# Ten steps later: when an expert stage makes its copies of x and gathers the next group

## The chip, the cores and the metric

One core of a Trainium2 chip runs the whole program. The metric is the device time of one execution in microseconds (us); where several runs were made, their median.

## The reference, cut to what matters

Two blocks follow each other on one sequence of 256 tokens with 1024 features, all in float32. The first block (two layers of neighbourhood and differential attention) is not touched. The second block has two layers:

```
for i in range(2):                       # layer 0: sparse attention, layer 1: latent attention
    proj = x @ w_in
    mix  = nsa_mixer(...) or mla_mixer(...)             # 12 heads
    xa   = memory_cross_attention(xq, mk, mv)           # 4 heads, 256 columns
    x    = layer_norm(ALPHA * x + concat(mix, xa) @ w_out[i])
    # 16 experts in 4 groups; each token goes to 2 of them
    f    = sum over experts e of gate_e * (silu(x @ w_gate[e]) * (x @ w_up[e])) @ w_down[e]
    x    = layer_norm(ALPHA * x + f)
```

One expert has w_gate and w_up (1024 x 512 each) and w_down (512 x 1024): 6 MiB of weights. Sixteen experts in two layers make 192 MiB, each byte read once.

## The kernel before, in words

**Order.** The order on TensorE (PE), VectorE (DVE) and ScalarE (ACT) is written out by hand. In the expert stage (`moe`) it goes by numbered steps: expert e has the sixteen steps from 16e, and at every odd step 16e + 2k + 1 the matmuls of feature block k (`Expert.mm(k)`, gate and up) are issued. `at(pre, s, fn)` puts other work ahead of step s, `at(post, s, fn)` behind it. Nothing waits for a step as such: each engine works through its own list and waits only for data and for free buffers.

**What stands around the experts.** Expert e's `gate1` to `hidden2` (ACT and DVE) run at 16e + 16 to 16e + 20, its two halves of `down` (PE) at 16e + 27 and 16e + 35, `result1` and `result2` at 16e + 37 and 16e + 38. Four experts share one group. For every group after the first, the tokens are gathered by matmul (`gather`, from `xs`, the two float32r parts of x, and from the one-hot matrices `Dg`, with four matmuls per feature block) into `xg`, and `back` makes `dT` and the gates. `hots` fills Dg in two calls. `x_parts` makes `xs` (one ACT copy and one DVE subtraction for each of four pieces of 128 x 512), from `xn`. `open_expert` puts the next group's pieces at steps counted from s = 16e of experts 2, 6 and 10.

**Buffers for weights.** The weights come in pieces of 512 KB, issued on the queue of SyncE (SP) into three kinds of buffers: `ring` (12 of one piece), `b8` (8 slots of two pieces) and `b4` (19 slots of one piece). b8 and b4 also hold the activations: xn, xg, xs, f are b8; Dg, dT, the experts' results ys are b4. When the last reader of a weight buffer has been issued, `Weights.read` frees it and, if `Weights.may` agrees, loads the next pieces of a fixed order into free slots at once. `may` looks ahead: `others` lists the steps at which the stage will take (+) or give back (-) slots for activations, and a free slot is refilled only if, at each of those steps, enough slots are free or come free (`last`, the step of a buffer's last reader) before it:

```
for s, n in self.others[kind]:
    if s >= self.step:
        free -= n
        if free + sum(e < s for e in ends) < 0:
            return False
```

In layer 0 the SP queue's order is the written one; in layer 1 SP is not in the hand-written schedule, and its loads are ordered by the framework's scheduler.

**The layer before the second expert stage** (`mla_layer`) goes by steps of another counter (`Flow`). The cross attention's result `xo` (128 x 2 x 256) is split into two float32r parts by `split_to` (one ACT copy, one DVE subtraction for each half) as feature blocks 6 and 7 of `yT`, which feeds the output projection.

Of the kernel before, what the change touches and what calls it, by code (L numbers as in the profile page):

```python
# [32 lines left out]
class Emit:  # L33


    def __init__(self, ctx, tc, aps, manual=False, nring=12, n8=8, n4=19, nw=3):
        self.tc, self.nc, self.a = tc, tc.nc, aps
        pool = lambda name, bufs, **kw: ctx.enter_context(tc.tile_pool(name=name, bufs=bufs, **kw))
        self.const = pool("const", 1)
        self.ring = pool("ring", nring)  # L40
        self.p8 = pool("p8", 1)
        self.p4 = pool("p4", 1)
        self.work = pool("work", 2)
        self.small = pool("small", 2)
        self.psum = pool("psum", 1, space=PSUM)
        self.slots = {"b8": list(range(n8)), "b4": list(range(n4)), "bank": list(range(8))}
        self.taken = {}
        self.lead = nw
        if manual:
            ctx.enter_context(tc.manual_schedule())  # L50
        nc = self.nc
        self.ident = self.const.tile([P, P], F32, name="ident")
        make_identity(nc, self.ident)
        self.sel = self.const.tile([P, 20], F32, name="sel")
        nc.vector.tensor_reduce(self.sel, self.ident.rearrange("p (j c) -> p c j", j=4)[:, :20], axis=AX.X, op=OP.add)
        self.mhalf = self.const.tile([P, 16], F32, name="mhalf")
        nc.vector.memset(self.mhalf, -0.5)
        self.one = self.const.tile([P, 1], F32, name="one")
        nc.vector.memset(self.one, 1.0)
# [1529 lines left out]
def mla_layer(E, x, f, st, flow, mkv, first, fill, W):  # L1589
# [3 lines left out]
    t = {}  # L1593
# [259 lines left out]
    for half in range(2):  # L1853
        s = 29 + 7 * half
# [9 lines left out]
    h0 = 34  # L1864
    yT = []
# [30 lines left out]
                                 m.pT[:, S * i:S + P * i], start=i == 0, stop=i == 1, skip_group_check=True)  # L1896
        E.free(*(m.pT for m in ms))

    def new_yT():
        yT.append(E.new_T("yT"))  # L1900
        for i in range(2):
            E.split_to(yT[0], 6 + i, t["xo"][:, i])
        E.free(t["xo"])

    flow.before(h0 + 8, new_yT)
    for j in range(6):
        ms = [Head(E, None, None, 2 * j + b, b, None) for b in range(2)]
        for m in ms:
            s = h0 + m.i
# [217 lines left out]
class Weights:  # L2127
# [3 lines left out]
    def __init__(self, E, i):  # L2131
        self.E, self.i, self.m = E, i, [E.a[n][i] for n in ("moe_w_gate", "moe_w_up", "moe_w_down")]
        self.pieces = {(e, w): [] for e in range(NE) for w in range(3)}
        self.order = []
        for e in range(NE):
            at = ((e, 0), (e, 1), *[(e - 2, 2)] * 2, *[(e, 0), (e, 1)] * 2, *[(e - 1, 2)] * 2, (e, 0), (e, 1))
            self.order += [p for p in at if p[0] >= 0 and p != (NE - 2, 2)]
        self.order += [(NE - 2, 2)] * 4 + [(NE - 1, 2)] * 4
        self.unread, self.ring = {}, []


        self.early = [(1, 0), (1, 0)]
        self.step, self.last = 0, {"b8": {}, "b4": {}}
        self.others = {"b8": [(28, 2), (64, -1), (88, 1)], "b4": [(11, 1), (13, -1)]}
        for s in (30, 94, 158):
            self.others["b4"] += [(s, 1), (s + 7, 1), (s + 19, 1), (s + 23, 1), (s + 30, -1), (s + 39, 1), (s + 55, 1)]
            self.others["b4"] += [(s + 62, -5)]
            self.others["b8"] += [(s + 69, 1), (s + 98, -1)]
        self.others["b4"] += [(226, 1), (229, 2), (232, 1), (235, 1), (238, -4), (245, 1), (257, 2)]
        if i == 0:  # L2150
            self.others["b8"].append((16 * NE - 19, 1))
            self.others["b4"].append((16 * NE - 19, 9))
        for v in self.others.values():
            v.sort(key=lambda e: (e[0], -e[1]))
# [207 lines left out]
def moe(E, x, i, W, st, columns, sums, tail=None, overflow=True):  # L2362
# [17 lines left out]
    def new_hots(m):  # L2380

        return E.b4((2, m, 2 * CAP), "Dg", F32R)

    def hots(Dg, slots, h, j=0, ts=range(2)):
        m = slots.shape[2]
        for t in ts:
            nc.vector.tensor_tensor(Dg[:, t, j:j + m, h * CAP:h * CAP + CAP],
                                    E.iota[:, None, :].to_broadcast([P, m, CAP]),
                                    slots[:, t, :, None].to_broadcast([P, m, CAP]), op=OP.is_equal)

    def new_group(m=n):

        return E.b8((KD, m, CAP), "xg"), []

    def new_back(g, m=n):
        ga = small.tile([P, n], F32, name="gall", tag="gall")
        g[1][:] = None, ga

        def new_dT():
            g[1][0] = E.b4((m, S), "dT", F32R)  # L2400
            return g[1][0]

        return new_dT, ga
# [6 lines left out]
    pre, post = {}, {}  # L2410

    def at(when, s, fn):
        when.setdefault(s, []).append(fn)

    def piece(s, gen, delay=2, m=1):

        def run():
            for k in range(m):
                out = next(gen)
                if delay:  # L2420
                    at(pre, s + delay + k, out)
                else:
                    out()
        at(post, s, run)

    groups, experts, ys = {}, {}, {}
    made = {}

    def open_expert(e):
        s, j, g = 16 * e, e % n, e // n  # L2430
        xg, matrices = groups[g]
        X = experts[e] = (Expert if e < NE - 1 else LastExpert)(E, [W.pieces[e, w] for w in range(3)], W.read, xg, j,
                                lambda: matrices[1][:, j:j + 1])
        if j == 2 and e + 2 < NE:
            slots = slot[:, :, e + 2:e + 2 + n]

            def start():
                made["Dg"] = new_hots(n)
                hots(made["Dg"], slots, 0)

            def gen():
                yield from gather(E, made["xs"], made["Dg"], groups[g + 1][0])
                yield from back(E, made["Dg"], E.gates, n * (g + 1), *new_back(groups[g + 1]))

            it = gen()
            at(pre, s - 2, start)
            at(pre, s + 3, lambda: groups.__setitem__(g + 1, new_group()))

            for d, m in ((3, 4), (17, 2)):
                piece(s + d, it, m=m)  # L2450
            at(pre, s + 14, lambda: hots(made["Dg"], slots, 1))
            at(post, s + 28, lambda: E.free(made["Dg"]))
        if j == n - 1:
            at(pre, s + 16, lambda: E.free(xg))
        if e == NE - 1:
            return
        for d, fn in ((16, X.gate1), (17, X.gate2), (18, lambda: X.hidden1(0)), (19, lambda: X.hidden1(1)),
                      (20, X.hidden2)):
            at(pre, s + d, fn)
        if e == NE - 2:  # L2460
            return
        for d in range(2):
            at(post, s + 27 + 8 * d, lambda d=d: X.down(d))
        at(pre, s + 37, X.result1)
        at(pre, s + 38, X.result2)
        at(pre, s + 39, lambda: ys.setdefault(g, []).append(X.y))
        if j == n - 1:
            def gen(f):
                yield from combine(E, f, ys.pop(g), matrices[0], range(n), None if g else made["xs"])

            def start():
                if g == 0:
                    made["f"] = E.b8((2, D), "f")
                it = gen(made["f"])
                piece(s + 44, it, m=4)
                at(post, s + 44, lambda: E.free(matrices[0]))

            at(pre, s + 40, start)

    with tc.manual_schedule(engines=ENGINES if i else ENGINES | {mybir.EngineType.SP}):  # L2480
# [3 lines left out]
        xn = E.b8((2, D), "xn")  # L2484
        negate, shift, choose, slots, gates1, gates2 = router(E, lg, mv, r, *sums)
# [6 lines left out]
        Dg = new_hots(n)  # L2492
# [32 lines left out]
        def x_parts(t, c):  # L2525
            if "xs" not in made:
                made["xs"] = E.b8((2, D), "xsh", F32R), E.b8((2, D), "xsl", F32R)
            hi, lo, src = (v[:, t, c] for v in (*made["xs"], xn))
            nc.scalar.copy(hi, src)
            nc.vector.tensor_sub(lo, src, hi)  # L2530
# [9 lines left out]
                at(pre, 9 + 2 * m + t, lambda t=t, c=c, j=j: gain(t, c, j))  # L2540
        for k in range(4):
            t, c = k % 2, slice(512 * (k // 2), 512 * (k // 2) + 512)
            at(pre, 28 + 0 * k, lambda t=t, c=c: x_parts(t, c))
        at(pre, 35, lambda: E.free(xn))

        ps, work = {}, ()

# [22 lines left out]
        for s in range(16 * NE + 2):  # L2570
            W.step = s
            e, k = divmod(s, 16)
# [57 lines left out]
    if overflow:  # L2630
        with tc.If(most > CAP, label=f"overflow{i}"):
            with tc.For_i(0, NE, 1) as e:
# [12 lines left out]
                for b in range(1, S // CAP):  # L2645
                    nc.vector.tensor_scalar(sl, sl, -float(CAP), None, op0=OP.add)
                    Dg = new_hots(1)
                    hots(Dg, sl, 0)
                    hots(Dg, sl, 1)
                    g = new_group(1)  # L2650
# [4 lines left out]
                    for w, k, c in ((wg, D, FF), (wu, D, FF), (wd, FF, D)):  # L2655
                        p = E.wload(rows(w, k) if c == D else rows8(w), k, c)
                        m = 1024 // c
# [101 lines left out]
def body(tc, aps, out):  # L2759
    nc = tc.nc  # L2760
    with ExitStack() as ctx:
# [17 lines left out]
        with tc.manual_schedule(engines=ENGINES):  # L2779
            x = E.b8((2, D), "x")  # L2780
            end = mla_layer(E, x, f, st, Flow(E, E.lead - 1), mkv, first, fill, W)
# [33 lines left out]
```

## Time and profile before

| what | us |
|---|---|
| median of 3 runs | 1001.55 |
| lowest, highest run | 998.66, 1002.4 |
| the profiled execution's own time | 998.92 |
| its span, first to last instruction | 997.2 |

The profiled execution lies 2.63 us below the median of the runs, and 1.72 us of its time lie outside the span. Times in the trace are counted from the span's start. Layer 0's expert stage runs from about 440 to 657 us, layer 1's from about 766 to 984. A busy share of PE in the profile is modelled: a matmul that stands waiting for its weights can count as busy, so the number of matmuls in a window tells more than its busy time.

### The profile page before, as it was taken

What the parts mean: (1) busy time and instruction counts of PE and PEld (TensorE: products, weight loads), DVE (VectorE), ACT (ScalarE), POOL (GpSimd) and SP (SyncE); (2) the same over time, 40 slices, a digit from 0 to 9 for tenths busy, and PEclk for the clock granted to TensorE, in tenths of its full rate; (3) what the DMA queues carried; (4) which work ended last, traced back from release to release, by engine and by line L of the source; (5) the groups of instructions that cost most, each with busy time, mean ns of one, the idle gap of its engine ahead of it and who ended that gap; (6) DMA issues with size and microseconds to landing.
All of it is one profiled execution on the core that took longest, in us unless ns stands there. A gap on an engine that the chain in (4) does not pass through costs nothing. (4 is left out here: it accounts for less than half of the span.)

```text
span 997.2 us, 16112 instructions
## 1 busy us (share of the span) xinstructions
PE 971.9 (97%) x5627; PEld 640.3 (64%) x5627; DVE 641.6 (64%) x1826; ACT 435.7 (44%) x1088; POOL 19.4 (2%) x40
## 2 busy tenths in 40 slices
PE   8999999999999989999999999999999999999995
PEld 8897889888897866775343443378867443434332
DVE  5857886557967788767456544467875645654455
ACT  6556664566664467653212121143875321212111
POOL 0000000000100000000000000000000000000000
PEclk9999999999999999999999999999999999999998
DMA  8963575443576584698999999977698899999995
GB/s 286 366 242 127 176 233 175 149 138 116 160 227 210 150 216 127 223 379 291 379 409 409 409 409 408 404 279 264 215 345 304 285 347 406 409 409 409 409 408 191
DMA packets 110889, 286.66 MB, mean 287 GB/s; under 512 B 14224, under 2 KB 30928, under 8 KB 110288
## 3 DMA queue, kind: packets, MB, share of 16 engines
q1 hardware_dynamic: 110800, 285.55, 79.8%
q8 instruction: 47, 0.77, 0.3%
q14 instruction: 42, 0.34, 0.1%
HBM read 284.46 MB, written 1.05 MB: 286 GB/s over the span
## 5 line engine op out<-in xcount | busy, mean ns | idle before, releaser
L2234 PE MATMUL eg<-wa,xg 128*64 128x512 f32 x792 | 204.9, 597 | 1.1 <-DMA wa<-moe_w_up_dram 0.8
L135 DVE TENSOR_TENSOR wsp<-w,wsp 128x512 fp32r<-128x512 f32 (+4 forms) x256 | 164.6, 656 | 64.0 <-ACT wsp L134 61.7
L253 PE MATMUL pj<-xTh,wsp 128*128 128x256 f32 x768 | 154.1, 291 | 1.7 <-ACT xTh L350 0.7
L134 ACT CAST wsp<-w 128x512 fp32r<-128x512 f32 (+4 forms) x256 | 142.3, 593 | 12.9 <-PE pj L253 5.7
L253 PEld LDWEIGHTS pj<-xTh,wsp 128*128 128x128 f32 x768 | 123.6, 191 | 9.0 <-issue 4.4
L2234 PEld LDWEIGHTS eg<-wa,xg 128*64 128x64 f32 x792 | 60.2, 137 | 107.1 <-issue 91.2
L2241 ACT ACTIVATE z<-eg 64x512 f32<-64x512 f32 x32 | 18.9, 592 | 210.2 <-PE eg L2234 210.2
L253 PE MATMUL pj<-xTl,wsp 128*128 128x256 f32 x384 | 108.6, 283 | 0.1
L253 PE MATMUL pj<-wsp,xTh 128*128 128x512 f32 (+3 forms) x352 | 108.5, 389 | 0.0
L2244 DVE SCALAR_TENSOR_TENSOR z<-z,eg 64x512 f32<-64x512 f32 x32 | 21.7, 679 | 127.6 <-ACT z L2241 127.6
L2254 DVE SCALAR_TENSOR_TENSOR hq<-z,gall,eg 32x128 f32<-32x128 f32 x240 | 83.4, 348 | 4.0
L2274 PE MATMUL dn<-wa,hT 128*64 128x512 f32 x348 | 83.8, 593 | 0.0
L253 PE MATMUL pj<-wsp,yTh 128*128 128x512 f32 x240 | 77.7, 405 | 0.0
L253 PEld LDWEIGHTS pj<-xTl,wsp 128*128 128x128 f32 x384 | 73.4, 191 | 0.7 <-DVE xTl L352 0.3
L2234 PE MATMUL eg<-w,xg 128*64 128x512 f32 x232 | 71.4, 595 | 0.2 <-DMA w<-moe_w_gate_dram 0.2
L253 PEld LDWEIGHTS pj<-wsp,xTh 128*128 128x128 f32 x352 | 62.8, 188 | 11.7 <-issue 2.5
L2285 ACT CAST ys<-dn 64x512 fp32r<-64x512 f32 x60 | 34.8, 580 | 75.5 <-PE dn L2274 65.5
L253 PE MATMUL pj<-wsp,xTl 128*128 128x512 f32 (+3 forms) x176 | 66.7, 379 | 0.0
L2274 PEld LDWEIGHTS dn<-wa,hT 128*64 128x64 f32 x348 | 24.7, 137 | 50.0 <-issue 42.7
L405 ACT ACTIVATE z<-z,mx 128x256 f32<-128x256 f32 (+1 forms) x104 | 48.1, 467 | 15.9 <-DVE mx L396 15.8
L2290 DVE TENSOR_TENSOR ys<-dn,ys 64x512 fp32r<-64x512 f32 x60 | 41.3, 689 | 12.3 <-ACT ys L2285 11.1
L253 PEld LDWEIGHTS pj<-wsp,yTh 128*128 128x128 f32 x240 | 43.1, 188 | 9.1 <-issue 1.6
(423 smaller groups left out, 1428.9 us busy)
## 6 DMA issues: line engine op xcount, KB each, us to landing
wa<-moe_w_up_dram SPq DMA_DIRECT2D x101, 512.0 KB, 10.2
wa<-moe_w_gate_dram SPq DMA_DIRECT2D x97, 512.0 KB, 10.2
wa<-moe_w_down_dram SPq DMA_DIRECT2D x93, 512.0 KB, 10.2
w<-w_in_dram SPq DMA_DIRECT2D x63, 512.0 KB, 5.0
w<-moe_w_down_dram SPq DMA_DIRECT2D x35, 512.0 KB, 10.2
w<-moe_w_gate_dram SPq DMA_DIRECT2D x31, 512.0 KB, 10.2
w<-moe_w_up_dram SPq DMA_DIRECT2D x27, 512.0 KB, 10.2
w<-w_out_dram SPq DMA_DIRECT2D x24, 512.0 KB, 3.6
```

Of the source, the lines that this page charges most:

```text
L134: self.nc.scalar.copy(hi, src)
L135: self.nc.vector.tensor_sub(lo, src, hi)
L253: nc.tensor.matmul(o, a, b, start=begin and i == 0, stop=last and i == 2, skip_group_check=True)
L405: E.nc.scalar.activation(z[i], (src or z)[i], AF.Exp, bias=mx[:, i:i + 1], scale=1.0 if src else -1.0, accum_out=sm[:, i:i + 1])
L2234: self.E.nc.tensor.matmul(self.ps[b * CAP:b * CAP + CAP], self.xg[:, k, self.j], w, start=k == 0, stop=k == KD - 1, skip_group_check=True)
L2241: self.E.nc.scalar.activation(self.th, self.ps[:CAP], AF.Tanh, scale=0.5)
L2244: self.E.nc.vector.scalar_tensor_tensor(self.th, self.th, 1.0, self.ps[:CAP], op0=OP.add, op1=OP.mult)
L2254: self.E.nc.vector.scalar_tensor_tensor(self.hq[32 * q:32 * q + 32, :, h], th[:, q], self.gate()[r], u[:, q], op0=OP.mult, op1=OP.mult)
L2274: self.E.nc.tensor.matmul(self.pd[n * CAP:n * CAP + CAP], self.hT[:, k], self.w[2][k](0)[:, 512 * n:512 * n + 512], start=k == 0, stop=k == 3,
L2285: self.E.nc.scalar.copy(self.y[r, n], self.pd[r])
L2290: self.E.nc.vector.tensor_sub(self.y[o, n], self.pd[r], self.y[r, n])
```

## The change

Three things move; no arithmetic changes, and the same instructions are issued.

- `x_parts`: the four pieces at step 28 go to steps 39, 40, 41 and 42, and xn is given back at 44, not 35.
- The next group's pieces (experts 2, 6, 10, steps from s = 16e): Dg taken and half filled at s + 10, not s - 2; xg taken at s + 13, not s + 3; the four gather pieces at s + 13, not s + 3; Dg's other half at s + 18, not s + 14; the two `back` pieces at s + 21, not s + 17; Dg given back at s + 22, not s + 28. The lists `others` follow.
- `mla_layer`: the two halves of xo are split at steps h0 + 7 and h0 + 9, not both at h0 + 8; yT's two b8 slots are taken one step earlier and xo's b4 slot is freed one step later.

```
-    def new_yT():
-        yT.append(E.new_T("yT"))
-        for i in range(2):
-            E.split_to(yT[0], 6 + i, t["xo"][:, i])
-        E.free(t["xo"])
-    flow.before(h0 + 8, new_yT)
+    def new_yT(i):
+        if i == 0:
+            yT.append(E.new_T("yT"))
+        E.split_to(yT[0], 6 + i, t["xo"][:, i])
+        if i == 1:
+            E.free(t["xo"])
+    for i in range(2):
+        flow.before(h0 + 7 + 2 * i, new_yT, i)
...
-        self.others = {"b8": [(28, 2), (64, -1), (88, 1)], "b4": [(11, 1), (13, -1)]}
+        self.others = {"b8": [(39, 2), (64, -1), (88, 1)], "b4": [(11, 1), (13, -1)]}
         for s in (30, 94, 158):
-            self.others["b4"] += [(s, 1), (s + 7, 1), (s + 19, 1), (s + 23, 1), (s + 30, -1), (s + 39, 1), (s + 55, 1)]
+            self.others["b4"] += [(s + 7, 1), (s + 12, 1), (s + 23, 2), (s + 24, -1), (s + 39, 1), (s + 55, 1)]
             self.others["b4"] += [(s + 62, -5)]
-            self.others["b8"] += [(s + 69, 1), (s + 98, -1)]
+            self.others["b8"] += [(s + 79, 1), (s + 98, -1)]
...
-            at(pre, s - 2, start)
-            at(pre, s + 3, lambda: groups.__setitem__(g + 1, new_group()))
-            for d, m in ((3, 4), (17, 2)):
+            at(pre, s + 10, start)
+            at(pre, s + 13, lambda: groups.__setitem__(g + 1, new_group()))
+            for d, m in ((13, 4), (21, 2)):
                 piece(s + d, it, m=m)
-            at(pre, s + 14, lambda: hots(made["Dg"], slots, 1))
-            at(post, s + 28, lambda: E.free(made["Dg"]))
+            at(pre, s + 18, lambda: hots(made["Dg"], slots, 1))
+            at(post, s + 22, lambda: E.free(made["Dg"]))
...
-            at(pre, 28 + 0 * k, lambda t=t, c=c: x_parts(t, c))
-        at(pre, 35, lambda: E.free(xn))
+            at(pre, 39 + k, lambda t=t, c=c: x_parts(t, c))
+        at(pre, 44, lambda: E.free(xn))
```

## Rows read from the trace of the kernel before

**Rows 1.** Windows of 25 us: stretch, PE, PEld, DVE, ACT, POOL busy, clock, DMA, GB/s.
```profile
575.00:600.00 25.00, 25.00 (x121) 8.95 (x121) 11.28 (x30) 5.29 (x11) 0.00 (x0) 1.00 1.03 409
600.00:625.00 25.00, 24.68 (x106) 9.81 (x104) 11.12 (x25) 4.42 (x8) 0.00 (x0) 1.00 1.03 409
625.00:650.00 25.00, 24.60 (x99) 8.74 (x96) 11.30 (x23) 3.59 (x7) 0.00 (x0) 1.00 1.03 397
...
950.00:975.00 25.00, 24.61 (x98) 9.05 (x98) 11.79 (x26) 4.64 (x8) 0.00 (x0) 1.00 1.03 405
```

**Rows 2.** PE's timeline late in layer 0's stage: start, length, what, idle before.
```profile
631.55 1.07 PE L2234 MATMUL eg<-wa,xg 128*64 128x512 f32 x2 [0.20 <-DMA wa<-moe_w_up_dram]
```

**Rows 3.** DMA issues from 495 to 640: count, KB, median us to landing.
```profile
DMA packets 16254, 59.27 MB, mean 409 GB/s; under 512 B 1804, under 2 KB 1804, under 8 KB 16245
...
wa<-moe_w_up_dram SPq DMA_DIRECT2D x24, 512.0 KB, 10.2
```

**Rows 4.** The SP queue's waits from 455 to 492: total us, times, longest.
```profile
SPq L2194 <- PE eg L2234: 18.2, 9, 5.7
```

**Rows 5.** Windows of 5 us, layer 0, columns as in Rows 1.
```profile
465.00:470.00 5.00, 5.00 (x24) 1.44 (x20) 3.41 (x10) 0.59 (x1) 0.00 (x0) 1.00 0.95 348
470.00:475.00 5.00, 5.00 (x40) 4.28 (x40) 3.50 (x8) 3.51 (x6) 0.00 (x0) 1.00 1.02 360
475.00:480.00 5.00, 5.00 (x26) 1.68 (x24) 0.00 (x0) 0.00 (x0) 0.00 (x0) 1.00 0.99 361
480.00:485.00 5.00, 5.00 (x28) 2.17 (x26) 3.05 (x8) 1.79 (x5) 0.00 (x0) 1.00 0.98 337
485.00:490.00 5.00, 5.00 (x26) 1.69 (x24) 2.58 (x9) 1.16 (x2) 0.00 (x0) 1.00 1.03 411
```

**Rows 6.** Windows of 5 us, layer 1, columns as in Rows 1.
```profile
790.00:795.00 5.00, 5.00 (x26) 1.64 (x24) 3.10 (x6) 2.77 (x5) 0.00 (x0) 1.00 0.94 316
795.00:800.00 5.00, 5.00 (x36) 3.56 (x33) 4.75 (x13) 2.34 (x4) 0.00 (x0) 1.00 0.79 270
800.00:805.00 5.00, 5.00 (x29) 2.26 (x29) 1.37 (x3) 1.17 (x2) 0.00 (x0) 1.00 0.90 267
805.00:810.00 5.00, 5.00 (x28) 2.14 (x26) 1.26 (x3) 1.32 (x4) 0.00 (x0) 1.00 1.02 379
810.00:815.00 5.00, 5.00 (x24) 1.61 (x24) 4.08 (x14) 1.63 (x4) 0.00 (x0) 1.00 0.96 302
```

**Rows 7.** DMA issues from 788 to 815, columns as in Rows 3.
```profile
wa<-moe_w_up_dram SPq DMA_DIRECT2D x5, 512.0 KB, 7.0
```

**Rows 8.** SP's timeline, layer 1: loads issued.
```profile
796.63 0.38 SPq L2194 DMA_DIRECT2D wa<-moe_w_gate_dram  x1
802.87 0.33 SPq L119 DMA_DIRECT2D w<-moe_w_down_dram  x1
...
814.37 0.33 SPq L2194 DMA_DIRECT2D wa<-moe_w_up_dram  x1
```

**Rows 9.** PE's timeline around layer 0's first gather (steps 35 to 43).
```profile
470.02 0.51 PE L2086 MATMUL xg<-Dg,xsh 128*128 128x256 f32 x2
...
474.05 3.65 PE L2234 MATMUL eg<-wa,xg 128*64 128x512 f32 x16
477.53 1.89 PE L2274 MATMUL dn<-wa,hT 128*64 128x512 f32 x8
```

**Rows 10.** DVE's timeline in the same stretch.
```profile
462.74 2.46 DVE L2530 TENSOR_TENSOR xsl<-xn,xsh 128x512 fp32r<-128x512 f32 x4
465.12 0.75 DVE L2387 TENSOR_TENSOR Dg<-iota,slot 128x256 fp32r<-128x256 f32 x2
...
471.46 1.39 DVE L2290 TENSOR_TENSOR ys<-dn,ys 64x512 fp32r<-64x512 f32 x2
```

**Rows 11.** Timeline at step h0 + 8 of layer 1's attention.
```profile
724.41 0.75 DVE L141 TENSOR_TENSOR yTl<-xo,yTh 128x256 fp32r<-128x256 f32 x2
...
725.71 0.61 PE L1883 MATMUL tp<-ident,z 128*128 128x128 f32 x3 [0.98 <-DVE z L164]
```

## The prediction

> **What bounds the kernel now.** I read the windows over the two expert stages first. In 575 to 600 PE issues 121 matmuls; after 600 it issues 106 and 99, and 98 late in layer 1, while memory stands at 409 GB/s [rows 1]. PE still looks 98% busy there, but its timeline shows matmuls that start behind a landing [rows 2]. So each stage ends on the weight stream: 512 KB at 409 GB/s are 1.28 us, and a landing 10.2 us after its issue is eight pieces in flight [rows 3]. In the second half of a stage nothing on PE, DVE or ACT moves the end; only an earlier stream does.
>
> Then I asked where the stream was late. Early in the stage the SP queue waits for PE to read a buffer before it may refill it: 18.2 us in nine waits from 455 to 492 [rows 4]. In that stretch memory is below its rate: 348, 360, 361, 337 GB/s in layer 0 until 485 [rows 5], and 316, 270, 267, 379, 302 in layer 1 until 815 [rows 6]. Afterwards it is full [rows 1, 5]. Against 409 the loss is (61 + 49 + 48 + 72) x 5 / 409 = 2.8 us in layer 0 and (93 + 139 + 142 + 30 + 107) x 5 / 409 = 6.2 us in layer 1. Whatever of this is recovered brings the end of the stage forward, as long as PE still waits at the end. How long it waits I estimate from the counts: (121 - 106 + 121 - 99) / 121 x 25 = 7.6 us in layer 0, an upper bound, since late work has other shapes; I take 5 us per layer as the cap.
>
> **The change, part by part.** *x's parts at 39, b8 slots.* The step promises two b8 slots for eleven steps more, but only if `may` can use them. I followed the fixed order of pieces by hand. In layer 0 the b8 weight tiles are read last at steps 11, 15, 19, 23, 59 and 63. The tiles of 19 and 23 were kept empty for xs at 28. Under the new list they stay empty until 39, since no other tile ends before 39. So in layer 0 this part frees nothing: 0. In layer 1 they end at 19, 27, 27, 35, 43 and 51. Before, both tiles of 27 stay empty and the tile of 35 is refilled; now one tile of 27 is refilled at once and the tile of 35 stays empty. Two pieces are issued eight steps earlier, and at 35 the count is the same again.
>
> *The later Dg, b4 slots.* In layer 0 one piece moves from step 39 to 31 (and one from 67 to 59, when the queue is full anyway). In layer 1 one moves from 35 to 23, one from 51 to 47, one from 63 to 55. Every one of these is a loan paid back within twelve steps.
>
> *The gather ten steps later.* It reads no weights and takes PE 474.05 - 470.02 = 4.0 us [rows 9]. Before, this pause lies ahead of step 37: in layer 1 the queue issues nothing from 796.63 to 802.87 [rows 8]. Now the reads of steps 37 to 45 come 4.0 us earlier and the pause lies ahead of 47. From 47 on PE is where it was (`back`, four steps later, gives step 51 some 2 us more), and the number of loads released is what it was.
>
> So the stream gains between the steps and is caught again by the same releases later. Ends of the estimate: nothing (caught wholly) and the whole loss (2.8 and 6.2 us). In layer 0 the reads after 485 already run at 411 GB/s [rows 5], so a piece gained there is kept: half of the bound, 1.4 us. In layer 1 releases still bind at 814.37 [rows 8], and a landing takes 7.0 us [rows 7], some five pieces; being ahead means fewer of them, and with a thin queue the rate was 267 to 302 [rows 6]. I take a quarter, 1.5 us. The later groups (steps 106 and 170) lie in the full stretch: 0; that cover is gone only if a stall there is longer than the eight pieces in flight, 10.2 us.
>
> *ACT and DVE at the new steps.* The x parts take DVE 2.46 us and half of Dg 0.75 [rows 10]. After the 1.39 us for ys, which ends at 472.85, they end at 472.85 + 2.46 + 0.75 = 476.06. PE reaches the moved gather after five blocks of mm (3.65 / 4 = 0.9 at most, 0.86 from start to start: (477.53 - 474.05) / 4 = 0.87) and one half down (1.7): 470.02 + 4.35 + 1.7 = 476.1 [rows 9, 10]. That is a tie. Bounds: 0, and 1 us a layer if ACT, which makes the high parts first, is late. I take 0.15 a layer, 0.3 in all. What queues behind x's parts on DVE is expert 2's hidden chain, which has until step 59.
>
> *xo in two steps.* DVE's two subtractions (0.75 us) at 724.41 stand before the scaling that PE waits 0.98 us for [rows 11]. Half of them goes a step earlier, where DVE is as full, and half a step later. Bounds: 0.75 saved, 0.4 lost; I take 0.4 saved. ACT's two copies move likewise and there the copy behind them waits for PE: 0.
>
> Sum: -1.4 - 1.5 + 0.3 - 0.4 = -3.0 us. Against the profiled execution's 998.92 that is 995.9; against the median of 1001.55, the number I forecast, 998.5.
>
> One rule speaks against any gain from the stream. The low windows stand at 337 to 361 GB/s in layer 0, the later ones at 409 [rows 5]. The Trainium skill's page "SBUF — State Buffer", section "Summary: rules for kernel authors", says to reckon with about 358 GB/s for transfers from HBM. By that the low windows of layer 0 would already be at memory's limit and its 1.4 us would be 0. This trace has 409 over 145 us [rows 3], so the rule doesn't hold here.
>
> **The rivals.**
> (1) *Caught wholly.* The loans are paid back and the same releases bind at steps 47 to 55; only xo and the tie are left: 0.1 us, 1001.4. For it: every moved load is repaid before the queue fills. Against it: rates in layer 0 are full directly afterwards.
> (2) *The stream keeps nearly all.* Layer 0 gives 2.8, layer 1 its cap of 5, xo 0.4: 8.2 us less, 993.3. For it: the queue's gap of 6.24 us [rows 8] goes just where memory is lowest. Against it: the pause is moved, not removed.
> (3) *Slower: the queue's head in layer 1.* SP's order there is the scheduler's. If it puts a piece whose slot is read after the moved gather ahead of pieces whose slots are free, all behind it wait. The longest wait for a read is 5.7 us [rows 4]; one such wait with no gain elsewhere costs 5.7 us, 1007.3. It decides from 3 us on, where it eats the forecast gain. Nothing in the trace shows that the order is disturbed by such shifts.
>
> **How the numbers follow.** Forecast 0.46, rival (1) 0.21, rival (2) 0.21, rival (3) 0.12. What a measurement can tell from no change is about 0.5%, 5.0 us. Faster by more: rival (2) and the far edge of the forecast (its layer 1 at 3.5 us), 0.27. Slower by more: three quarters of rival (3), 0.09. Within: 0.64. The range runs from 993.5 (nearly all of rival 2) to 1002.5 (rival 1 with a gather that stalls 1 us in one layer); outside lie most of rival (3) and the far end of rival (2), 0.2 together.
>
> **What would show it.** Right: layer 0's windows from 465 to 485 rise towards 409, layer 1's low windows move from 795 to 805 towards 805 to 815, and both stages' last loads land 1 to 2 us earlier relative to the stage's start. The wait ahead of the z transpose in attention shrinks from 0.98 to about 0.5. Wrong: low windows of the same total somewhat later and an unmoved end (rival 1); 409 from 790 on (rival 2); an SP wait of 4 us or more for a read while memory is low in layer 1 (rival 3). A gather that starts with a wait for DVE or ACT of over 1 us would make the tie wrong.

## The result, and the profile after

The changed kernel takes 1011.16 us (median of 6 runs, 1010.5 to 1014.05), the kernel before 1001.62 (6 runs). The ratio is 1.0104, 95% interval 1.0087 to 1.0122: slower by 10.4 us, 8.7 to 12.2 (the ratio is that of the means; the medians lie 9.5 us apart). The profiled execution of the changed kernel took 1011.59, its span is 1009.9 us, 12.7 longer than that of before.

The loss has one place. The waits of PE from 650 to 672 us name it (total us, times, longest):

```profile
PE dn L2320 <- SPq L2633: 10.7, 1, 10.7
```

PE's timeline around it:

```profile
655.97 1.08 PE L2320 MATMUL dn<-w,hT 128*64 128x256 f32 x8
656.98 0.74 PE L2615 MATMUL sum<-ys,dT 128*128 128x256 f32 x4
668.45 1.97 PE L2320 MATMUL dn<-wa,hT 128*64 128x256 f32 x8 [10.73 <-SPq L2633]
...
672.72 1.53 PE L1000 MATMUL mkv<-memT,wkv 128*128 128x256 f32 x4
674.09 0.59 PE L1004 MATMUL mkv<-wkv,memT 128*128 128x256 f32 x2
```

Before, the same work reads:

```profile
656.13 0.74 PE L2613 MATMUL sum<-ys,dT 128*128 128x256 f32 x4
656.79 1.08 PE L2318 MATMUL dn<-wa,hT 128*64 128x256 f32 x8
...
660.22 0.59 PE L1004 MATMUL mkv<-wkv,memT 128*128 128x256 f32 x2
```

The matmul that waits is the last quarter of the last expert of layer 0. The releaser named is a branch on SP's queue. What was really late is seen in SP's timeline, after and (second fence) before:

```profile
641.34 5.68 SPq L119 DMA_DIRECT2D w<-moe_w_down_dram  x3
647.07 1.18 SPq L982 DMA_DIRECT2D memT<-memT_dram  x1
648.36 3.10 SPq L119 DMA_DIRECT2D wkv<-mem_w_kv_dram  x4
651.72 6.13 SPq L119 DMA_DIRECT2D w_in<-mla_w_in_dram  x4
658.59 0.60 SPq L119 DMA_DIRECT2D wa<-moe_w_down_dram  x1
```

```profile
639.26 2.93 SPq L119 DMA_DIRECT2D w<-moe_w_down_dram  x3
643.05 4.39 SPq L119 DMA_DIRECT2D wa<-moe_w_down_dram  x2
647.55 2.03 SPq L982 DMA_DIRECT2D memT<-memT_dram  x1
649.62 2.36 SPq L119 DMA_DIRECT2D wkv<-mem_w_kv_dram  x4
652.39 6.07 SPq L119 DMA_DIRECT2D w_in<-mla_w_in_dram  x4
```

Before, the last two weight pieces go out ahead of the next layer's nine loads (memT, four wkv, four w_in). Now the very last piece stands behind all nine, is issued 14.7 us after the one before it and lands at 668.41, where PE starts. `moe` puts the nine loads on the queue at step 16 NE - 19 = 237, whatever has been loaded by then; before, the last refill was that of step 235, now it is that of step 239.

The windows of 5 us show what follows the wait (columns as in rows 1):

```profile
655.00:660.00 5.00, 2.72 (x18) 1.75 (x18) 2.55 (x7) 0.37 (x1) 0.00 (x0) 1.00 1.04 384
660.00:665.00 5.00, 0.00 (x0) 0.00 (x0) 0.00 (x0) 0.00 (x0) 0.00 (x0) 0.51 0.96 336
665.00:670.00 5.00, 1.55 (x8) 0.77 (x8) 0.00 (x0) 0.00 (x0) 0.00 (x0) 0.50 0.14 47
670.00:675.00 5.00, 4.85 (x19) 3.90 (x18) 2.42 (x8) 0.37 (x1) 0.36 (x1) 0.63 0.42 112
675.00:680.00 5.00, 5.00 (x28) 4.39 (x27) 2.19 (x4) 2.83 (x6) 0.34 (x1) 1.00 1.07 374
```

While PE stands, the granted clock is at the lower level, 0.50, and it stays there for some 5 us of the work behind: the eight matmuls at 668.45 take 1.97 us, those at 655.97 took 1.08. Set against before, the two traces lie 0.85 us apart ahead of the wait (656.98 and 656.13), 11.66 at its end (668.45 and 656.79) and 13.87 where the full clock is back (674.09 and 660.22): 10.8 us of waiting and 2.2 of slow clock, 13.0 together. That is more than the whole loss. The rest of the kernel is a little faster.

What answers to the low windows of layer 1 [rows 6], each 14 us later, as that stage begins 14.18 later (770.92 to 785.10):

```profile
804.00:809.00 5.00, 5.00 (x26) 1.84 (x26) 0.59 (x1) 0.59 (x1) 0.00 (x0) 1.00 0.99 327
809.00:814.00 5.00, 5.00 (x27) 1.59 (x24) 4.75 (x13) 2.77 (x6) 0.00 (x0) 1.00 1.02 406
814.00:819.00 5.00, 5.00 (x31) 2.76 (x28) 3.11 (x6) 1.16 (x3) 0.00 (x0) 1.00 0.92 332
819.00:824.00 5.00, 5.00 (x33) 3.06 (x33) 1.10 (x3) 1.72 (x4) 0.00 (x0) 1.00 0.95 318
824.00:829.00 5.00, 5.00 (x28) 2.17 (x26) 4.79 (x12) 2.67 (x7) 0.00 (x0) 1.00 0.97 353
```

Their sum is 1736 against 1534, the largest gain (406 against 270) where the gather stood, and the dip is now where it stands (332, 318). Five windows flatter the change: with the two ahead of them and the one behind the sums are 2698 against 2589, 109 more, or 109 x 5 / 409 = 1.3 us; the window behind fell from 413 to 334, so a part of the gain is only moved. In layer 0 [rows 5] the same four windows read 292, 379, 351 and 418, 34 more in sum. But the two ahead of them read 491 in sum where they read 556 before, and the stage begins 1.58 us later here, so layer 0's windows show no gain. SP waits less for the matmuls of gate and up between 455 and 492 [rows 4] (all its waits for PE there: 25.0 us, 29.0 before):

```profile
SPq L2196 <- PE eg L2236: 12.6, 8, 4.3
```

The moved gather of layer 0 starts without a wait, just as the work ahead of it on DVE ends (PE, then DVE) [rows 9, 10]:

```profile
477.62 0.53 PE L2088 MATMUL xg<-Dg,xsh 128*128 128x256 f32 x2
...
474.48 2.50 DVE L2532 TENSOR_TENSOR xsl<-xn,xsh 128x512 fp32r<-128x512 f32 x4
476.89 0.75 DVE L2389 TENSOR_TENSOR Dg<-iota,slot 128x256 fp32r<-128x256 f32 x2
```

### The profile page after: what moved, and what is told of

The parts are those of the page before. It is cut to its first block, busy times and chain, and to the rows that moved or that the text cites. A ratio compares the mean times of both kernels' runs of the same rounds, so it can differ in the third digit from the quotient of the medians.

```text
span 1009.9 us, 16113 instructions
## 1 busy us (share of the span) xinstructions
PE 972.6 (96%) x5627; PEld 642.3 (64%) x5627; DVE 641.8 (64%) x1826; ACT 434.1 (43%) x1088; POOL 19.3 (2%) x40
## 5 line engine op out<-in xcount | busy, mean ns | idle before, releaser
L2236 PE MATMUL eg<-wa,xg 128*64 128x512 f32 x780 | 200.3, 596 | 0.6 <-DMA wa<-moe_w_gate_dram 0.4
L134 ACT CAST wsp<-w 128x512 fp32r<-128x512 f32 (+4 forms) x256 | 142.5, 593 | 12.2 <-PE pj L253 5.9
L2276 PE MATMUL dn<-wa,hT 128*64 128x512 f32 x364 | 86.5, 593 | 1.9 <-DVE hT L2264 1.9
L2236 PE MATMUL eg<-w,xg 128*64 128x512 f32 x244 | 75.7, 596 | 0.2 <-DMA w<-moe_w_up_dram 0.2
L253 PE MATMUL pj<-wsp,yTl 128*128 128x512 f32 x120 | 47.1, 392 | 0.0
## 6 DMA issues: line engine op xcount, KB each, us to landing
wa<-moe_w_gate_dram SPq DMA_DIRECT2D x98, 512.0 KB, 10.2
wa<-moe_w_up_dram SPq DMA_DIRECT2D x97, 512.0 KB, 10.2
wa<-moe_w_down_dram SPq DMA_DIRECT2D x96, 512.0 KB, 10.2
w<-moe_w_down_dram SPq DMA_DIRECT2D x32, 512.0 KB, 10.2
w<-moe_w_up_dram SPq DMA_DIRECT2D x31, 512.0 KB, 10.2
```

What stands on the lines that cost most here:

```text
L134: self.nc.scalar.copy(hi, src)
L253: nc.tensor.matmul(o, a, b, start=begin and i == 0, stop=last and i == 2, skip_group_check=True)
L2236: self.E.nc.tensor.matmul(self.ps[b * CAP:b * CAP + CAP], self.xg[:, k, self.j], w, start=k == 0, stop=k == KD - 1, skip_group_check=True)
L2276: self.E.nc.tensor.matmul(self.pd[n * CAP:n * CAP + CAP], self.hT[:, k], self.w[2][k](0)[:, 512 * n:512 * n + 512], start=k == 0, stop=k == 3,
```

## The experiments

Theory Q: the last piece of layer 0 is late because it stands behind nine loads in one queue, and that costs everything and more. Rival G: the later group work costs the time inside the stage, and the piece is late only because all is. Theory P, formed after the first six runs, says why the piece comes so late.

### 1. The nine loads two steps later

```
-            if tail and not work and s == 16 * NE - 19:
+            if tail and not work and s == 16 * NE - 17:
```

> The changed kernel with one number altered: the next layer's nine loads (memT, four wkv, four w_in) are put on the SP queue behind step 239 instead of behind step 237. Theory Q (the last weight piece of layer 0 stands behind those nine loads, its landing is what PE waits 10.73 us for, and the slow clock after the wait costs 2.2 us more): the piece is issued directly behind the one before it (about 645 us on the trace), PE's wait at the last quarter is under 2 us, and the time falls by 10.7 + 2.2 = 12.9 us to 998.3, or 999.6 if memT and wkv, now 1.3 us later, become late themselves. Rival G (the later gather and x parts cost the time somewhere in the stage, and the piece is only late because everything is): stays within 2 us of 1011.2.

999.74 us, ratio to before 0.9981 (0.9967 to 0.9995). One number takes back 11.4 us by the medians (12.3 by the two ratios), and what is left of the change is faster than before. The order of the queue and PE's last quarter:

```profile
641.56 5.72 SPq L119 DMA_DIRECT2D w<-moe_w_down_dram  x3
647.33 1.19 SPq L119 DMA_DIRECT2D wa<-moe_w_down_dram  x1
648.57 2.09 SPq L982 DMA_DIRECT2D memT<-memT_dram  x1
```

```profile
657.84 1.08 PE L2320 MATMUL dn<-wa,hT 128*64 128x256 f32 x8
```

The piece is issued 2 us later than expected and lands at 656.39, 1.45 us ahead of its use. It is still loaded at step 239, so the late step alone costs nothing: what costs is the place in the queue. Theory Q stands; rival G falls.

### 2. The last two pieces held back, in the kernel before

```
-            while self.order and self.E.slots[kind] and self.may(kind):
+            while self.order and self.E.slots[kind] and self.may(kind) and (self.i, self.step) != (0, 235):
```

> The kernel before, with nothing of the change; the refill of step 235, which loads the last two pieces of layer 0, is held back to the next refill at step 239, so that both go behind the next layer's nine loads. Theory Q: the two pieces are issued at about 657 and 658.5 us, PE waits from 655.1 until the first lands at about 667, 12 us, and the slow clock costs 2 us more: 1015.6 in the median, 1013 in a profiled execution like the one of before. Rival G: the group work of before is untouched, so no more than the late landing's own slack, under 3 us: at most 1004.

1016.1 us in one run, PE's wait 11.19 us. The queue's order alone makes this loss, with none of the change's other parts:

```profile
668.51 1.97 PE L2318 MATMUL dn<-wa,hT 128*64 128x256 f32 x8 [11.19 <-DMA wa<-moe_w_down_dram]
```

### 3. The group pieces alone

x's parts at step 28 and xo in one step as before; from the change only this, and xn given back at 44:

```
+            at(pre, s + 10, start)
+            at(pre, s + 13, lambda: groups.__setitem__(g + 1, new_group()))
...
-        at(pre, 35, lambda: E.free(xn))
+        at(pre, 44, lambda: E.free(xn))
```

> Of the change only the later group pieces (Dg, xg, gather, back ten steps later, with their slots); x's parts at step 28 and xo in one step as before, and xn's slot is given back at step 44 so that xg can have it at 45. The order of the loads worked out by hand ends with one piece refilled at step 239 here too. Theory Q: a wait of 10 to 11 us at the last quarter of layer 0 and 1009 to 1013 us. A rival X, by which x's parts at 39 to 42 cost the time (DVE and ACT ahead of the moved gather): about 1001.

1010.98 us in one run, PE's wait 11.11. The group pieces with their slots are enough for the loss; no share of x's parts at 39 shows.

### 4. xo alone

The kernel before with `new_yT(i)` at h0 + 7 and h0 + 9, as in the change.

> Of the change only xo's split in two steps. The prediction's term: 0.4 us less, 1001.2. What the changed kernel's trace suggests: the z transpose in attention begins 0.3 us later against its neighbours, so 0.3 us more, 1001.9. Neither is more than a median can show; what counts is PE's wait ahead of that transpose, 0.98 us before: about 0.5 by the prediction, about 1.3 by the trace after.

1001.8 us, ratio 1.0005 (0.9996 to 1.0014): nothing that the median can show. The traces can: from the last mkv matmul to the first gather of layer 1 it takes 63.57 to 63.60 us in the six kernels with xo in one step (before, 2, 3, 5, 6, 8) and 63.91 to 63.95 in the five with two (after, 1, 4, 7, 9). So it costs 0.33 us. The wait of 0.98 us [rows 11] did not shrink to 0.5 and did not grow to 1.3; a second one came (waits of PE from 700 to 790, before and then here):

```profile
PE tp L1883 <- DVE z L164: 1.0, 1, 1.0
```

```profile
PE tp L1883 <- DVE z L164: 1.4, 2, 1.0
```

DVE's timeline here says why the first half brought nothing:

```profile
724.86 0.43 DVE L141 TENSOR_TENSOR yTl<-xo,yTh 128x256 fp32r<-128x256 f32 x1 [0.51 <-ACT yTh L140]
```

The half that moved a step earlier waits 0.51 us for its own copy on ACT, more than the 0.37 us (half of 0.75) that were moved out of the next step; and the half that moved a step later stands ahead of the next scaling, where the new wait of 0.41 us is.

### 5. Experiment 1 with xo in one step

> The kernel of the first experiment (the change, with the next layer's nine loads behind step 239) with xo split in one step again, as before. Against the first experiment the stretch from the last mkv matmul to the first gather of layer 1 shrinks from 63.92 to 63.60 us, as in the kernels without the xo part, so 0.3 us less in all: 999.4, ratio to before about 0.998. If the xo part had helped elsewhere, it would be above 999.74.

998.74 us, ratio 0.9975 (0.9962 to 0.9988). The stretch is 63.60 us. It is the fastest kernel of the study by its median; against experiment 1 the difference (1 us) is within the intervals.

### 6. The kernel before, with the nine loads two steps later

> The kernel before, with nothing of the change, and the next layer's nine loads behind step 239 instead of 237. Its last pieces are issued at step 235 either way, so the order of the queue stays as it was. Theory Q with the prediction's stream: no change, within 0.5 us of before, both expert stages as long as before (layer 1 about 202 us from the first to the last gate and up matmul). Rival: the 2 us that the first experiment gained come from the later loads themselves and not from the group work; then 999.7 here too.

1001.32 us, ratio 1.0006 (0.9994 to 1.0018). So what experiments 1 and 5 gain on the kernel before does not come from the later loads; what is left of the change is the moved work in the expert stages.

### 7. Without the slot kept for a group that doesn't exist

Why is the last refill that of step 239? The list of slots to be kept runs over s = 30, 94 and 158. For s = 158 it keeps a two-piece slot for an xg at s + 79 = 237, but after the fourth group there is none to come. Experiment 7 leaves that out of the changed kernel:

```
-            self.others["b8"] += [(s + 79, 1), (s + 98, -1)]
+            self.others["b8"] += [(s + 79, 1), (s + 98, -1)] if s < 158 else []
```

> The changed kernel, the nine loads behind step 237 as in it; only the list of slots to be kept differs: the two-piece slot that the list keeps for a group of tokens after the fourth (s = 158, step 237, given back at 256), which no group ever takes, is left out. Theory P (that claim keeps a free two-piece slot empty until a buffer of its kind is released at step 239, so the last piece finds no place before the nine loads): followed by hand the last piece is issued at step 235; PE's wait at the last quarter is under 2 us and the time that of the first experiment, 999.7. Rival: the last piece is late for another reason (the ring or the one-piece slots); then about 1011.

999.02 us, ratio 0.9986 (0.9973 to 0.9998), with the nine loads at step 237. All pieces now go ahead of them, and PE has no wait at the last quarter:

```profile
638.58 8.19 SPq L119 DMA_DIRECT2D w<-moe_w_down_dram  x5
646.82 2.09 SPq L982 DMA_DIRECT2D memT<-memT_dram  x1
```

### 8. The same with xo in one step

> The kernel of the run before this one, with xo split in one step as before the change. 0.3 us less than that one, 998.7 to 999.4, the same as the fifth experiment's 998.74 if nothing else binds; lower if the slot that is now in use in both layers also brings the stream forward.

999.39 us, ratio 0.9990 (0.9977 to 1.0003). The stretch of xo is 63.60 again, but the median is 0.4 us above experiment 7's: a part of 0.3 us is below what medians of this kernel can order. The slot that is now in use brings no further gain that shows.

### 9. The claim at step 227, as before the change

```
+            self.others["b8"] += [(s + 79, 1), (s + 98, -1)] if s < 158 else [(s + 69, 1), (s + 98, -1)]
```

> The changed kernel with that claim at step 227, where it was before the change. A slot is only refilled when a buffer of its kind is released, and by hand none of the two-piece kind is released between 227 and 239 here; so theory P has the last piece at 239 and 1009 to 1013 us although the claim has run out. A rival, by which the claim's step (237 against 227) is what decides: about 999.7.

1013.17 us in one run, the piece again behind the nine:

```profile
652.46 5.36 SPq L119 DMA_DIRECT2D w_in<-mla_w_in_dram  x4
658.55 0.61 SPq L119 DMA_DIRECT2D wa<-moe_w_down_dram  x1
```

So it is not the step of the claim that decides. A slot kept empty is looked at again only when a buffer of its kind is released. Worked out from the planner's code, step by step for layer 0: in the kernel before, two-piece buffers are released at steps 195, 199 and 235, and 235 takes the last two pieces. With the moved groups the pieces fall into other buffers, and the releases are those of 195, 199, 203 and then 239. The slots of 199 and 203 are kept empty, one for memT and one for the group that doesn't exist, and nothing of the kind is released until 239. In experiment 7 the slot of 199 is refilled at once, and the last piece goes out at 235. Theory P stands: kept empty for nobody, and not looked at in time.

## Why the prediction was wrong, step by step

**What bounds the stage.** Right, as far as the runs show. From 495 to 640 us the changed kernel reads at 409 GB/s too, and the stages with the moved groups are shorter. The length of a stage from its first to its last gate and up matmul, from the traces (kernels 7 and 8 left out, as a slot more is in use there):

```
                                     layer 0                            layer 1
groups as before (before, 2, 4, 6)   202.51 201.96 201.51 202.20        201.91 202.90 201.92 201.35
groups later (after, 1, 3, 5, 9)     201.73 201.55 201.15 200.34 201.83 201.04 200.67 201.09 201.52 201.18
means                                202.05 -> 201.32                   202.02 -> 201.10
```

**The stream terms,** -1.4 and -1.5 us: right in sign, -0.7 and -0.9 by these means, between the forecast and rival (1). The size is uncertain: the single traces of a group differ by up to 1.6 us, and a slow clock delays the first gate matmul (last section) and shortens the length so measured. Counted from the first gather instead, the means fall by 0.8 and 0.5. What the prediction expected to see shows in layer 1: 45 us after the stage's first gate matmul 64 of its weight pieces have landed in each of the four kernels with the groups as before, 65 or 66 in the five with the groups later, and at 100 us 106 against 107. So of two pieces gained one is kept, and one piece is 1.28 us. In layer 0 the counts of the two groups overlap at both times (63 to 64 and 64 to 65; 105 to 106 and 106 to 108). That repaid loans took the rest was not tested.

**x's parts,** 0 in layer 0: right. By the planner's code experiment 3, which has them at 28, loads the same pieces at the same steps of layer 0 as the changed kernel, and its stages (201.15, 201.09) are no longer than those with them at 39.

**The gather's tie,** +0.3: 0 measured. DVE ends at 476.89 + 0.75 = 477.64 and PE begins at 477.62, 1.5 us later than worked out, as all of this stage is (444.06 to 445.64); PE waits for nothing, in layer 1 neither.

**xo,** -0.4: wrong in sign, +0.33. The step assumed that half of DVE's work leaves the tight step and left out that the moved half waits for ACT's copy there.

**The step that failed** is the sentence "The later groups (steps 106 and 170) lie in the full stretch: 0; that cover is gone only if a stall there is longer than the eight pieces in flight". It looked for a stall at those steps. One did come, of 0.97 us in each layer (in the changed kernel at 526.71 and 866.17), in each of the seven kernels with later groups and in none of the four without: the gather used to give DVE the time to finish expert 5's `hidden2`, and now `down` waits for it. It is far shorter than the 10.2 us in flight, and no cost of it shows. But the later groups moved something else: which piece goes into which buffer, and so at which step the last one is loaded. The order of the pieces was followed by hand to step 67 and left there, as if every loan were paid back. By the planner's code it is not: in layer 0 the changed kernel is two pieces ahead from step 67 to 103 and two behind at 107, and behind step 235 it has one piece left where the kernel before has none. Everything needed was in the code and the trace of before. The code puts the nine loads at step 237, two steps behind the last refill, and the last weight piece goes out just ahead of memT (646.26 and 647.55). The nine are one of 1024 KB, four of 512 and four of 416 (sizes and counts of the whole run of before; memT is loaded once more elsewhere):

```profile
memT<-memT_dram SPq DMA_DIRECT2D x2, 1024.0 KB, 7.7
wkv<-mem_w_kv_dram SPq DMA_DIRECT2D x4, 512.0 KB, 10.8
w_in<-mla_w_in_dram SPq DMA_DIRECT2D x4, 416.0 KB, 11.2
```

That is 4736 KB, at 409 GB/s 11.9 us, less the 1.5 us by which that piece landed ahead of its use (655.28 and 656.79): 10.4 us of wait. Measured in the changed kernel were 12.3 us from the landing of the piece before the nine to that of the last of them (654.69 to 666.99), and 10.7 of wait.

**Rival (3)** had the mechanism, a load at the queue's head or behind others that PE waits for, but sought it in layer 1, because SP's order there is the scheduler's. It came in layer 0, where the order is the written one and a late piece can't be taken ahead. Its price, 5.7 us, was half (the view it was taken from has a wait for a read of 6.4 us too, in another row), and the 2.2 us of slow clock after a long wait of PE stood in no term. Its sign, a wait of SP of 4 us or more in layer 1, could not tell: the longest is 5.0 us from 800 to 835, and 5.8 in the same stretch before.

**The sum.** -0.7 - 0.9 + 0.3 + 13.0 = +11.7 us, where 10.4 (8.7 to 12.2) were measured. Without the queue's part -1.3 remains; experiment 1 measured -1.9 (-0.5 to -3.3). The forecast's -3.0 lies inside that interval, near its far end.

## What to carry to other kernels

When slots or claims of a planner move, follow its order of loads to the last piece, not to the next step at which the counts agree again; what stands on the same queue at a fixed step behind it makes the difference between 1.5 us of slack and 10 us of wait. The price can be worked out beforehand: the bytes of the loads ahead of it at the rate of the stream, less the slack, and the time at the lower clock after it. And look for claims that nobody takes: the one here showed no harm until the order shifted (the kernel before without it was not run).

## What the hardware showed unasked

Early in layer 0's expert stage the granted clock is not the same from execution to execution. Before and in experiment 6 PE runs the same instructions up to there, with the same idle stretch of 0.82 us ahead of the first gather (439.95 and 439.70); the windows that follow, before and then experiment 6:

```profile
440.00:442.00 2.00, 2.00 (x20) 1.96 (x20) 1.55 (x7) 2.00 (x2) 0.00 (x0) 1.00 1.00 387
442.00:444.00 2.00, 2.00 (x19) 1.92 (x17) 0.91 (x4) 0.69 (x3) 0.00 (x0) 1.00 1.03 385
```

```profile
440.00:442.00 2.00, 2.00 (x13) 1.94 (x13) 0.78 (x4) 1.80 (x2) 0.00 (x0) 0.50 1.03 410
442.00:444.00 2.00, 2.00 (x11) 2.00 (x11) 1.45 (x6) 0.00 (x0) 0.00 (x0) 0.50 1.03 410
```

At the upper level (1.00, 2.4 GHz) it is 4.10 us from the first gather to the first gate matmul, at the lower (0.50, 1.2 GHz) 6.60. Nine of the eleven profiled executions show the lower level there for a while; that of before and experiment 3 don't. The Trainium skill, page "TensorE: Matmul & The Clock Gate", section "Part 1: The HAM clock gate", says that the number of slow matmuls at a kernel's start differs from run to run of one kernel; these traces show such a difference inside the kernel, of 2.5 us between the two.

The times go with it. Of the 66 runs of the kernel before that were taken beside the experiments, nineteen had a mean granted clock of 0.989 and a median of 1002.3 us, five had 0.994 and 998.74. The profiled execution of before had 0.994, and lay 2.63 us under its median. So a single profile can lie some us beside its kernel's median by the clock alone; that no other cause has a share was not tested.
